# A list scheduler that knows a shared port, and gains moved from weights to activations

## The chip, the cores and the metric

The kernel runs on one core of one Trainium2 chip. Its engines work side by side, each with its own list of instructions in a fixed order: TensorE (PE) multiplies matrices, VectorE (DVE) and ScalarE (ACT) work on whole tiles, GpSimd (POOL) does the same more slowly, and SyncE (SP) issues the transfers. Instructions of different engines wait for each other by semaphores. The metric is the device time of one execution in microseconds (us). Lower is better.

## The reference

Two layers of a hybrid decoder over 1024 tokens of width 1024. Each layer normalises `x`, projects it once for four groups of heads, mixes, normalises each group, projects back, and then runs a gated feed-forward part of inner width 2816:

```python
def rmsnorm(x, gain):
    y = xf * lax.rsqrt(jnp.mean(xf * xf, axis=-1, keepdims=True) + NORM_EPS)
    return (y * gain.astype(jnp.float32)).astype(x.dtype)
...
for l in range(DEPTH):
    h = rmsnorm(x, norm_mix[l])
    (a_x, a_gate, b_q, b_kv, b_gate, c_q, c_k, c_v, c_glr, c_og,
     d_cq, d_ckv, d_kr) = jnp.split(h @ w_in[l], offsets, axis=-1)
    y_a = rglru_mixer(...); y_b = nsa_mixer(...)
    y_c = gla_mixer(...);   y_d = mla_mixer(...)
    y = jnp.stack([y_a, y_b, y_c, y_d], axis=2)
    y = rmsnorm(y, group_norm[l].reshape(N_GROUPS, GROUP_WIDTH)).reshape(B, S, MIX_WIDTH)
    x = x + y @ w_out[l]
    h = rmsnorm(x, norm_ffn[l])
    gate, up = jnp.split(h @ w_gate_up[l], 2, axis=-1)
    x = x + (jax.nn.silu(gate) * up) @ w_down[l]
return rmsnorm(x, final_norm)
```

`rglru` is a gated linear recurrence, `nsa` an attention over compressed, selected and recent keys, `gla` linear attention with a decay for each channel, `mla` attention with low-rank queries and keys.

## The kernel before

Everything is kept in tiles of 128 partitions; the 1024 tokens are eight tiles `t`. Matrix products in full precision are made of three passes: each operand is split in a rounded part and the rest (two instructions, a cast on ScalarE and a subtraction on VectorE, which writes `T`, `w`, `wu` or `h`), and three of the four products are summed in PSUM.

**Stages of a layer.** Start: `norm_stream` computes `hn` (the normalised tile, without the gain) on VectorE, TensorE transposes it (L464), and the first columns of `w_in` are applied (L607). Linear attention: `gla_levels` multiplies, for each tile and each of four levels, a decayed query `dq` with a mask of the heads into `Qz`, and for a fifth level into `Qb`; TensorE then forms the scores (L938, L935). Beside that other columns of `w_in` fill TensorE (L607). Then the stage of the sparse attention's keys: `blk` are the blocks of keys with a position vector added, for the compression (L1164), `ckvn` the normalised low-rank key, `kd` a rotated key that TensorE transposes (L1061, L1089). Then both attentions, the output projection (L1787) with the residual additions `x_res`, and the feed-forward part. That one saves products by forming sums and differences of blocks of weights and activations first (`utmp`, `qtmp`, `hn`, `h1`, `h6`, `h7`, on GpSimd and VectorE): its entry transposes the normalised `hn` (L1934), its long products are L2158, and the down projection is L2299 with the last piece in L2324.

**Gains.** A group of weights (`Weights`) may carry a gain; `refine` then multiplies the loaded tile `stg` by it on GpSimd, `stg<-stg,gn`, before it is split (for the group that is needed first, inside the split on ScalarE and VectorE). This holds the gain of the first norm for `w_in` and that of the group norms for `w_out`. The feed-forward norm applies its gain in the norm itself: `hn<-x_res,rstd,ps`, with the gain's row broadcast in a PSUM tile. The power -1/2 of each norm is a GpSimd instruction, `rstd<-ms,negh`.

**What sets the order.** The program runs through `Flow`, a list scheduler at build time. Streams (generators) yield the time from which they can go on; each instruction has a cost by hand for its engine: `D_` for VectorE, `P_` for GpSimd, `A_` for ScalarE, `f.pe` for TensorE. `run` takes whatever can start first on its clock and writes it out, so the engines' orders follow from these costs. `when` adds a fixed delay between two engines. Nothing in this clock ties VectorE to GpSimd. Nearly all instructions are recorded at one line, L254.

```python
    def run(self, until):
        while not until():
...
            for eng, q in self.ops.items():
                c = self.clk.get(eng, 0.0)
                for o in q:
                    r = when(o[3], eng)
...
                    key = (max(c, r + load), o[0], r, o[1])
...
                start = max(self.clk.get(eng, 0.0), key[2])
...
                self.clk[eng] = o[7].t = start + o[2]
```

## Time and profile before

| | us |
|---|---|
| three runs, median | 2597.49 |
| lowest, highest | 2597.26, 2599.34 |
| the profiled execution | 2599.47 |
| its span | 2597.7 |

| engine | busy us | share of the span |
|---|---|---|
| TensorE, matmul | 2515.2 | 97% |
| TensorE, weight load (overlaps) | 2129.9 | 82% |
| VectorE | 1925.3 | 74% |
| ScalarE | 1248.9 | 48% |
| GpSimd | 870.9 | 34% |

The mean granted clock of TensorE is 0.991. A high share of one engine says what bounds the kernel on average; where that engine stands idle is read from the stretches and from the timeline. A number in square brackets behind an instruction in the timeline is the idle time of its engine just before it, with what ended that. An instruction that is marked x2 or x3 is a row of that many.

### The profile page before, as it was taken

The numbers are of one execution on the slowest core, as the hardware profiler recorded it, in microseconds if no ns is written. First come the engines' busy times: TensorE is split into PE (matmuls) and PEld (weight loads), VectorE is DVE, ScalarE is ACT, GpSimd is POOL, SyncE is SP. The second block draws the span as 40 slices with busy tenths as digits, with TensorE's granted clock in tenths as the row PEclk, the third lists the DMA queues.
The fourth block names the chain that finished last, engine by engine and source line by source line (L and its number), as shares of the span: only waits on it lengthen the run. The fifth ranks groups of instructions, "written<-read, shape, count | busy, mean of one in ns | idle before, by whom it ended". The sixth has DMA issues, their size and how long they took to land. (4 is left out here: it accounts for less than half of the span.)

```text
span 2597.7 us, 37861 instructions
## 1 busy us (share of the span) xinstructions
PE 2515.2 (97%) x13502; PEld 2129.9 (82%) x13502; DVE 1925.3 (74%) x3668; ACT 1248.9 (48%) x2791; POOL 870.9 (34%) x820
## 2 busy tenths in 40 slices
PE   9999999998999999999999999999989999999998
PEld 8788978887888888778888888888878888887786
DVE  7976987787665665798769678867875665667976
ACT  5444577774333333444343455877653333334443
POOL 4530122233333333543225211222243333336522
PEclk9999999999999999999999999999999999999999
DMA  3011102212223323543310111031302323335522
GB/s 132 27 37 58 42 17 80 60 61 71 86 91 108 106 99 100 213 156 98 114 60 17 53 47 36 25 90 46 107 28 94 106 99 101 105 104 204 162 90 89
DMA packets 136556, 222.12 MB, mean 86 GB/s; under 512 B 13456, under 2 KB 83504, under 8 KB 133808
## 3 DMA queue, kind: packets, MB, share of 16 engines
q1 hardware_dynamic: 136368, 219.70, 25.7%
q8 instruction: 107, 1.75, 0.3%
q14 instruction: 81, 0.66, 0.1%
HBM read 161.99 MB, written 49.28 MB: 81 GB/s over the span
## 5 line engine op out<-in xcount | busy, mean ns | idle before, releaser
L2158 PE MATMUL ps<-T,wu 128*128 128x512 f32 (+1 forms) x2160 | 498.8, 386 | 1.0 <-DVE qtmp L254 0.9
L2158 PEld LDWEIGHTS ps<-T,wu 128*128 128x128 f32 x2160 | 400.7, 189 | 85.4 <-issue 1.3
L2158 PE MATMUL ps<-h,wu 128*128 128x512 f32 (+1 forms) x1656 | 386.4, 386 | 1.1 <-ACT ps L254 0.6
L2158 PEld LDWEIGHTS ps<-h,wu 128*128 128x128 f32 x1656 | 302.2, 188 | 70.0 <-ACT ps L254 0.8
L607 PE MATMUL ps<-w,T 128*128 128x256 f32 x2304 | 314.8, 291 | 8.2 <-DVE ckvn L254 5.7
L607 PEld LDWEIGHTS ps<-w,T 128*128 128x128 f32 x2304 | 290.2, 192 | 17.0 <-issue 9.7
L2299 PE MATMUL ps<-T 128*128 128x512 f32 x1176 | 275.6, 390 | 3.8 <-DVE x_res L254 3.8
L254 POOL TENSOR_TENSOR rstd<-ms,negh 128x1 f32<-128x1 f32 (+1 forms) x152 | 98.8, 651 | 510.7 <-DVE ms L254 495.8
L2299 PEld LDWEIGHTS ps<-T 128*128 128x128 f32 x1176 | 220.8, 188 | 52.4 <-DVE x_res L254 4.3
L254 POOL TENSOR_TENSOR utmp<-stg,stg 128x512 f32<-128x512 f32 x84 | 113.9, 1356 | 340.5 <-DVE wu L254 134.5
L254 ACT CAST wu<-stg 128x512 fp32r<-128x512 f32 x220 | 136.2, 619 | 190.1 <-PE ps L2158 80.2
L254 DVE TENSOR_TENSOR wu<-utmp,wu 128x512 fp32r<-128x512 f32 x134 | 109.9, 820 | 110.9 <-ACT wu L254 104.4
L1787 PE MATMUL ps<-w,T 128*128 128x512 f32 x768 | 190.9, 396 | 0.0
L254 DVE TENSOR_TENSOR wu<-stg,wu 128x512 fp32r<-128x512 f32 x214 | 178.7, 836 | 14.8 <-ACT wu L254 14.8
L254 DVE TENSOR_TENSOR x_res<-x_res,ps 128x512 f32<-128x512 f32 x224 | 143.4, 680 | 31.5 <-PE ps L2299 16.3
L1787 PEld LDWEIGHTS ps<-w,T 128*128 128x128 f32 x768 | 140.3, 188 | 26.8
L254 DVE TENSOR_TENSOR pts<-ps,pts 128x512 fp32r<-128x512 f32 x212 | 139.4, 685 | 21.2 <-ACT pts L254 20.6
L254 ACT CAST wu<-utmp 128x512 fp32r<-128x512 f32 x134 | 83.2, 621 | 115.6 <-POOL utmp L254 115.4
L254 POOL TENSOR_TENSOR stg<-stg,gn 128x1024 f32<-128x1024 f32 x48 | 94.6, 1978 | 130.4 <-DMA stg<-in_w_out_dram 59.8
L254 POOL TENSOR_TENSOR stg<-stg 128x512 f32<-128x512 f32 x88 | 130.0, 1497 | 3.5
L254 ACT CAST pts<-ps 128x512 fp32r<-128x512 f32 x212 | 117.4, 586 | 21.7 <-PE ps L1711 17.1
L254 POOL TENSOR_TENSOR utmp<-stg 128x512 f32<-128x512 f32 x48 | 67.6, 1409 | 175.2 <-DMA stg<-in_w_gate_up_dram 79.5
(380 smaller groups left out, 4927.4 us busy)
## 6 DMA issues: line engine op xcount, KB each, us to landing
stg<-in_w_gate_up_dram SPq DMA_DIRECT2D x88, 512.0 KB, 3.8
stg<-af SPq DMA_DIRECT2D x70, 512.0 KB, 3.6
af<-so SPq DMA_DIRECT2D x20, 1024.0 KB, 6.1
stg<-in_w_in_dram SPq DMA_DIRECT2D x36, 512.0 KB, 3.7
br<-in_w_down_dram SPq DMA_DIRECT2D x24, 512.0 KB, 6.2
af<-sg SPq DMA_DIRECT2D x20, 512.0 KB, 2.7
stg<-in_cmp_w_dram SPq DMA_DIRECT2D x16, 512.0 KB, 3.9
stg<-in_w_out_dram SPq DMA_DIRECT2D x16, 512.0 KB, 3.7
```

The lines of the kernel that those rows point to most:

```text
L254: o[4](*o[5], **o[6])
L607: PE.matmul(o[:, :256], lhsT=T[:, a, k, t * P:(t + 1) * P], rhs=g.of(k)[:, b, :], start=(k == 0 and i == 0), stop=(k == NK - 1 and i == 2))
L1787: PE.matmul(o, lhsT=T[:, a, 2 * u + k, t * P:(t + 1) * P], rhs=w.w[:, b_, k * 512:k * 512 + 512], start=(n == 0), stop=(n == 6 * len(us) - 1))
L2158: PE.matmul(bk[b, i][:, cs], lhsT=u[:, x, k * P:(k + 1) * P], rhs=H[n][:, y, k, cs], skip_group_check=True, start=(start and k == 0 and s ...
L2299: PE.matmul(o, lhsT=a[:, x, t * P:(t + 1) * P], rhs=b[:, y], skip_group_check=True, start=(new and s == 0), stop=(k == k0 + nk - 1 and s = ...
```

## The change

It has three parts. First, the scheduler's clock. Delays between engines follow the engine that finishes (`LAG`) and the one that waits (`MORE`); matmuls cost `mm(n)` or, in fp32, `mm4(n)`, in the place of constants by hand; a scan costs twice as much as before; and instructions of VectorE and GpSimd that use the port between them (`two` in `D_`, every `tensor_tensor` in `P_`) start on the clock only when the other engine's last such instruction is over. Second, the products `Qz` and `Qb` in `heads` go from GpSimd to VectorE. Third, the gains leave the weights: `refine` multiplies nothing, and the norm applies the gain in one `scalar_tensor_tensor` with a gain row that is loaded broadcast over the partitions (`gain_rows`; `gm` for the first norm, `grow` for the group norms). For this SP issues a load of 512 KB behind the first tile of `x`, and others later; the host stores `group_norm` in another order.

```diff
+LAG = {"DVE": 0.12, "ACT": 0.14, "POOL": 0.08, "PE": 0.19}
+MORE = {"PE": 0.03, "POOL": 0.06}
-        return x.t + (0.12 if x.eng == eng else 0.26 if eng == "PE" else 0.19)
+        return x.t + LAG.get(x.eng, 0.19) + MORE.get(eng, 0.0)
+def mm(n):
+    return (n + 32) / 2400
+def mm4(n):
+    return max(n / 1200 + 0.003, 0.112)
...
                     r = when(o[3], eng)
+                    if o[10]:
+                        r = max(r, self.port["POOL" if eng == "DVE" else "DVE"])
...
                 self.clk[eng] = o[7].t = start + o[2]
+                if o[10]:
+                    self.port[eng] = start + o[2]
...
     def D_(n, deps, func, *a, **k):
-        return f.do("DVE", 0.07 + n / 960, deps, func, a, k)
+        name = getattr(func, "__name__", "")
+        two = (name in ("tensor_tensor", "tensor_tensor_scan") and sbuf(a[1]) and sbuf(a[2])
+               or name == "scalar_tensor_tensor" and sbuf(a[1]) and sbuf(a[3])
+               or name in ("tensor_scalar", "tensor_copy") and sbuf(a[0]) and sbuf(a[1]) and n >= 64)
+        return f.do("DVE", 0.07 + n / 960, deps, func, a, k, None, two)
...
-                e = P_(n, [e, par["ev"]], G.tensor_tensor, sv, sv, g.unsqueeze(2).to_broadcast([P, k, n // k]),
-                       ALU.mult)
...
-        return r, P_(172, e, G.tensor_tensor, r[:, :n], ms[:, :n], negh[:, :n], ALU.pow)
+        return r, P_(172 if n == 1 else 400, e, G.tensor_tensor, r[:, :n], ms[:, :n], negh[:, :n], ALU.pow)
+    def gain_rows(g, src):
+        nc.sync.dma_start(g, src.partition_broadcast(P))
+        return g, f.dma(P * DM * 2)
...
-            tn = D_(600, e, V.tensor_scalar, hn, src, r[:, 0:1], None, ALU.mult)
+            tn = D_(1024, [e, gain[1]], V.scalar_tensor_tensor, hn, src, r[:, 0:1], gain[0], ALU.mult, ALU.mult)
...
-            te = f.pe(6 * 0.216)
+            te = f.pe(6 * mm(512))
...
             if t == 0:
+                gmix.extend(gain_rows(gp.tile([P, DM], F32, name="gm"), I["norm_mix"][0]))
                 f.add(params(0, par), 0, "par")
...
         def heads(Q, src, n, deps):
-            return P_(4 * n, deps, G.tensor_tensor, Q, src.unsqueeze(1).to_broadcast([P, 4, n]),
+            return D_(4 * n, deps, V.tensor_tensor, Q, src.unsqueeze(1).to_broadcast([P, 4, n]),
                       bdmask.unsqueeze(2).to_broadcast([P, 4, n]), ALU.mult)
...
-            e = D_(160, e, V.tensor_scalar, yn, y, r[:, 0:1], None, ALU.mult)
+            e = D_(256, [e, A["ggrp"][1]], V.scalar_tensor_tensor, yn, y, r[:, 0:1], A["ggrp"][0][:, grp // 2],
+                   ALU.mult, ALU.mult)
```

TensorE keeps its 1975 rows of the program; GpSimd goes from 615 to 487, VectorE from 3277 to 3304. Three places show what moves.

GpSimd in linear attention of layer 0, before (`Qz`, `Qb` are the products with the heads' mask, `stg` a weight tile) and then of the change (`ms`, `rstd` are the norms' mean squares and powers):

```order
L254 TENSOR_TENSOR Qz0_921<-dq_1083,bdmask_105 128x256
L254 TENSOR_TENSOR Qb_924<-d_1099,bdmask_105 128x512
L254 TENSOR_TENSOR stg_1112<-stg_1112,gn_128 128x1024
L254 TENSOR_TENSOR Qz1_922<-dq_1156,bdmask_105 128x256
L254 TENSOR_TENSOR Qz2_923<-dq_1173,bdmask_105 128x256
L254 TENSOR_TENSOR stg_1131<-stg_1131,gn_128 128x1024
L254 TENSOR_TENSOR Qz0_921<-dq_1210,bdmask_105 128x256
L254 TENSOR_TENSOR Qz1_922<-dq_1216,bdmask_105 128x256
L254 TENSOR_TENSOR Qz2_923<-dq_1265,bdmask_105 128x256
L254 TENSOR_TENSOR Qb_924<-d_1259,bdmask_105 128x512
```

```order
L275 MEMSET wbd_894 128x512
L275 TENSOR_TENSOR rstd_1380<-ms_1379,negh_94 128x4
L275 TENSOR_TENSOR rstd_1383<-ms_1382,negh_94 128x1
L275 TENSOR_TENSOR rstd_1532<-ms_1531,negh_94 128x4
L275 TENSOR_TENSOR rstd_1535<-ms_1534,negh_94 128x1
L275 TENSOR_TENSOR rstd_1707<-ms_1706,negh_94 128x4
L275 TENSOR_TENSOR rstd_1710<-ms_1709,negh_94 128x1
L275 TENSOR_TENSOR rstd_1885<-ms_1884,negh_94 128x4
L275 TENSOR_TENSOR rstd_1888<-ms_1887,negh_94 128x1
```

The products and the gain multiplications are gone from GpSimd's row, and the small powers stand one behind the other.

VectorE at the entry of the feed-forward part of layer 0, before and then of the change, from the last subtraction of the tile before to the norm of the last tile that TensorE transposes:

```order
L254 TENSOR_TENSOR stg3_7670<-ps_8018,hn_7732 128x512
L254 TENSOR_TENSOR h6_7680<-hn_7732,h6_7680 128x4x128
L254 TENSOR_TENSOR T_108<-stg3_7670,T_108 128x4x128 x2
L254 TENSOR_TENSOR h1_7684<-hn_7732,h1_7684 128x4x128
L254 TENSOR_TENSOR x_res_7532<-x_res_7532,ps_7976 128x512
L254 TENSOR_TENSOR h7_7676<-hn_7732,h7_7676 128x4x128
L254 TENSOR_TENSOR wu_8062<-stg_7749,wu_8062 128x512
L254 TENSOR_TENSOR wu_8074<-stg_7690,wu_8074 128x512
L254 TENSOR_TENSOR x_res_7532<-x_res_7532,ps_8040 128x512
L254 TENSOR_SCALAR ms_8083<-ss_8082 128x1
L254 TENSOR_TENSOR wu_8062<-utmp_7675,wu_8062 128x512
L254 SCALAR_TENSOR_TENSOR hn_7732<-x_res_7532,rstd_8084,ps_7726 128x1024
```

```order
L275 TENSOR_TENSOR stg3_7566<-ps_7937,hn_7651 128x512
L275 TENSOR_TENSOR x_res_7468<-x_res_7468,ps_7899 128x512
L275 TENSOR_TENSOR T_108<-stg3_7566,T_108 128x4x128 x2
L275 TENSOR_TENSOR h1_7580<-hn_7651,h1_7580 128x4x128
L275 TENSOR_SCALAR ms_7985<-ss_7984 128x1
L275 TENSOR_TENSOR x_res_7468<-x_res_7468,ps_7965 128x512
L275 TENSOR_TENSOR h7_7572<-hn_7651,h7_7572 128x4x128
L275 TENSOR_TENSOR wu_7989<-stg_7630,wu_7989 128x512
L275 SCALAR_TENSOR_TENSOR hn_7651<-x_res_7468,rstd_7986,ps_7615 128x1024
```

The first `x_res` has moved ahead of two `T` and `h1`, and of the `wu` additions one is left ahead of `hn` instead of three.

VectorE at the entry of the down projection of layer 0, before and then of the change, from the `x_res` additions (four of one group, of which the second piece shows the last two) to the `wu<-utmp` that TensorE's first product with that tile waits for:

```order
L254 TENSOR_TENSOR x_res_7532<-x_res_7532,ps_10995 128x512
L254 TENSOR_TENSOR x_res_7532<-x_res_7532,ps_11001 128x512
L254 TENSOR_TENSOR T_108<-utmp_7675,T_108 128x512
L254 TENSOR_TENSOR x_res_7532<-x_res_7532,ps_11008 128x512
L254 TENSOR_TENSOR x_res_7532<-x_res_7532,ps_11014 128x512
L254 TENSOR_TENSOR wu_8062<-stg_11019,wu_8062 128x512
L254 TENSOR_TENSOR T_108<-qtmp_7674,T_108 128x512
L254 TENSOR_TENSOR T_108<-stg3_7670,T_108 128x512 x2
L254 TENSOR_TENSOR T_108<-stg_11041,T_108 128x512
L254 TENSOR_TENSOR wu_8074<-utmp_7675,wu_8074 128x512
```

```order
L275 TENSOR_TENSOR x_res_7468<-x_res_7468,ps_10930 128x512
L275 TENSOR_TENSOR x_res_7468<-x_res_7468,ps_10936 128x512
L275 TENSOR_TENSOR T_108<-utmp_7571,T_108 128x512
L275 TENSOR_TENSOR wu_7989<-stg_10926,wu_7989 128x512
L275 TENSOR_TENSOR T_108<-stg3_7566,T_108 128x512
L275 TENSOR_TENSOR T_108<-qtmp_7570,T_108 128x512
L275 TENSOR_TENSOR T_108<-stg3_7566,T_108 128x512
L275 TENSOR_TENSOR T_108<-stg_10972,T_108 128x512
L275 TENSOR_TENSOR T_108<-utmp_7571,T_108 128x512
L275 TENSOR_TENSOR wu_7993<-stg_11019,wu_7993 128x512
L275 TENSOR_TENSOR T_108<-qtmp_7570,T_108 128x512
L275 TENSOR_TENSOR wu_7993<-utmp_7571,wu_7993 128x512
```

The four `x_res` now stand together, and behind them come one `T<-utmp`, one `wu<-stg` and one `T<-qtmp` more than before, all ahead of this `wu<-utmp` (the other `T<-utmp` stood among the `x_res` before).

## Rows read from the trace of the kernel before

**Rows 1.** The page, part 1: busy us (share of the span) xinstructions, by engine.

```profile
PE 2515.2 (97%) x13502; PEld 2129.9 (82%) x13502; DVE 1925.3 (74%) x3668; ACT 1248.9 (48%) x2791; POOL 870.9 (34%) x820
```

**Rows 2.** Waits of PE: line, releaser: us in total, times, longest us.

```profile
PE ps L2299 <- DVE wu L254: 7.9, 2, 4.0
...
PE ps L938 <- POOL Qz L254: 4.7, 8, 1.2
```

**Rows 3.** Stretches of 40 us: sum, busy per engine (xcount), PEclk, DMA share, GB/s.

```profile
40.00:80.00 40.00, 38.75 (x221) 31.68 (x221) 31.54 (x97) 18.51 (x45) 12.96 (x13) 1.00 0.20 60
80.00:120.00 40.00, 37.46 (x233) 30.92 (x232) 37.42 (x111) 14.48 (x64) 22.66 (x27) 1.00 0.03 10
680.00:720.00 40.00, 40.00 (x175) 32.63 (x174) 24.65 (x32) 12.77 (x22) 14.00 (x10) 1.00 0.30 99
1440.00:1480.00 40.00, 39.15 (x221) 32.34 (x220) 32.23 (x66) 19.74 (x42) 12.65 (x13) 1.00 0.10 34
```

**Rows 4.** Lines by form, GpSimd: shapes xcount | busy us, mean ns | idle before.

```profile
L254 POOL TENSOR_TENSOR stg<-stg,gn 128x1024 f32<-128x1024 f32 x48 | 94.6, 1978 | 130.4 <-DMA stg<-in_w_out_dram 59.8 <-DMA stg<-in_w_in_dram 48.1 <-DVE x_res L254 21.4
...
L254 POOL TENSOR_TENSOR Qz<-dq,bdmask 128x256 f32<-128x256 f32 x64 | 43.6, 685 | 72.5 <-DVE dq L254 48.4 <-PE ps L814 18.3 <-PE ps L607 3.2
```

**Rows 5.** Lines by form, VectorE, same columns.

```profile
L254 DVE SCALAR_TENSOR_TENSOR hn<-x_res,rstd,ps 128x1024 f32<-128x1024 f32 x16 | 20.4, 1278 | 5.1 <-POOL rstd L254 4.9
...
L254 DVE TENSOR_TENSOR kd<-k,kt 128x256 f32<-128x256 f32 x16 | 6.7, 417 | 0.0
...
L254 DVE TENSOR_SCALAR hn<-x_res,rstd 128x1024 f32<-128x1024 f32 x8 | 6.0, 748 | 0.1
```

**Rows 6.** Timeline in linear attention: start us, us, instruction.

```profile
81.01 2.04 POOL L254 TENSOR_TENSOR stg<-stg,gn 128x1024 f32<-128x1024 f32 x1 [1.02 <-ACT d L254]
...
81.22 1.99 DVE L254 TENSOR_TENSOR d<-b 128x128 f32<-128x128 f32 x1
```

**Rows 7.** Timeline of the start stage.

```profile
22.57 2.38 DVE L254 TENSOR_SCALAR hn<-xt,rstd 128x1024 f32<-128x1024 f32 x1
...
25.09 1.06 PE L464 MATMUL ps<-ident,hn 128*128 128x128 f32 x8 [2.20 <-DVE hn L254]
```

**Rows 8.** Timeline of the stage behind linear attention.

```profile
247.15 2.02 DVE L254 TENSOR_TENSOR blk<-X,par 128x504 f32<-128x504 f32 x2
...
249.70 1.62 PE L607 MATMUL ps<-w,T 128*128 128x256 f32 x6 [2.85 <-DVE ckvn L254]
...
259.26 4.52 POOL L254 TENSOR_TENSOR stg<-stg,gn 128x1024 f32<-128x1024 f32 x2
...
259.60 5.08 DVE L254 TENSOR_TENSOR blk<-X,par 128x504 f32<-128x504 f32 x2
...
267.25 0.30 PE L1089 MATMUL ps<-ident,kd 128*128 128x128 f32 x1 [1.75 <-DVE kd L254]
```

**Rows 9.** Timeline at the entry of the feed-forward part.

```profile
636.38 3.49 DVE L254 TENSOR_TENSOR T<-stg,T 128x512 fp32r<-128x512 f32 x2
...
640.39 0.68 DVE L254 TENSOR_TENSOR x_res<-x_res,ps 128x512 f32<-128x512 f32 x1
...
644.58 1.28 DVE L254 SCALAR_TENSOR_TENSOR hn<-x_res,rstd,ps 128x1024 f32<-128x1024 f32 x1 [0.44 <-POOL rstd L254]
...
646.00 1.94 PE L1934 MATMUL ps<-ident,hn 128*128 128x128 f32 x8 [5.82 <-DVE lamw L254]
```

**Rows 10.** The stretch of 40 us there, columns as in Rows 3.

```profile
640.00:680.00 40.00, 32.07 (x191) 28.36 (x191) 31.38 (x69) 19.19 (x37) 17.26 (x13) 0.91 0.13 40
```

**Rows 11.** Timeline at the entry of the down projection.

```profile
1096.94 4.02 DVE L254 TENSOR_TENSOR T<-stg,T 128x512 fp32r<-128x512 f32 x3
1097.09 1.64 POOL L254 TENSOR_TENSOR qtmp<-br 128x512 f32<-128x512 f32 x1 [0.63 <-DVE T L254]
...
1100.88 0.68 DVE L254 TENSOR_TENSOR wu<-utmp,wu 128x512 fp32r<-128x512 f32 x1
...
1101.61 4.71 PE L2299 MATMUL ps<-wu,T 128*128 128x512 f32 x11 [3.94 <-DVE wu L254]
```

More of the change, by code (lines that the diff above doesn't have):

```diff
@@ L535, in params, with norm_stream @@
                    cpos=pr[:, 21:53].rearrange("p (j lp) -> p j lp", j=2), s4n=s4n, s2p=s2p,
-                   halfb=halfb, wg2=wg2, glan=glan, done=e)
-    def norm_stream(ready, load, hp, bufs, done, ahead=NT):
+                   halfb=halfb, glan=glan, done=e)
+    def norm_stream(ready, load, gain, hp, bufs, done, ahead=NT):
         hs = Slots(bufs)
@@ L620, in start_stage @@
         evs = []
-        f.add(norm_stream(ready, load, hp, bufs, done, 1), 4, "start")
+        f.add(norm_stream(ready, load, gain, hp, bufs, done, 1), 4, "start")
         def evac(t, o, te):
```

147 lines of the change are left out of this document (76 added, 71 removed).

## The prediction

> **What bounds the kernel now.** I read the page's first part, then TensorE's busy share by stretches of 40 us, then TensorE's waits, and then the timeline at each place where it stood idle. TensorE is busy 2515.2 us of a span of 2597.7 [rows 1], so all its idle time together is 2597.7 - 2515.2 = 82.5 us. The change gives TensorE the same 1975 rows of work in another order, so everything to be won or lost lies in those 82.5 us and in the clock. In the long matrix products of the feed-forward part a stretch of 40 us holds 40.00 us of matmul [rows 3]: nothing can be won there, whatever VectorE and GpSimd do. The idle time lies at the joints: the start, linear attention, the stage behind it, the entry of the feed-forward part, the entry of the down projection, and the tail. At most of them the releaser is VectorE, and beside the late VectorE instruction stands a GpSimd instruction.
>
> That is the second thing to see. A VectorE subtraction of 128x128 took 1.99 us while GpSimd multiplied a 128x1024 weight tile by its gain for 2.04 us [rows 6], though a product of twice that size on VectorE takes 0.417 us [rows 5]. Behind linear attention two additions `blk` took 2.02 us by themselves and 5.08 us beside two gain multiplications of 4.52 us [rows 8]. The two engines do not overlap there; one stands behind the other. The Trainium skill says so too: SBUF — State Buffer, section "Who interferes with whom", has a VectorE instruction with two SBUF inputs and a GpSimd instruction that reads SBUF exclude each other for the whole instruction. The trace agrees with the times just given. The rule also speaks against one part of the change: a product moved to VectorE still has two SBUF inputs, and by the rule alone it would go on standing behind GpSimd; the sum would then hold +7 instead of -7 for linear attention, and be +3.5. The order of the change shows only small powers left on GpSimd there, so I keep this as a rival.
>
> **Gains leave the weights.** 48 multiplications on GpSimd go, 94.6 us of its time [rows 4]. GpSimd is busy only 34% [rows 1], so its own time is worth nothing; what counts is which VectorE instruction stood behind one of them where TensorE waited. I take the places one by one.
>
> Start: the norm of a tile took 2.38 us where an undisturbed one of the same form takes 0.748 [rows 5, 7], and TensorE then stood idle 2.20 us [rows 7]. Up to 2.38 - 0.75 = 1.6 us goes. Against it, the fused norm (with the gain in the same instruction) is dearer: the nearest row is the fused form of the feed-forward norm, 1.278 us against 0.748 [rows 5], so 0.53 us on the first tile's chain, and the load of the broadcast gain is queued on SP ahead of the first weights. I take -1 us, between -2 and +2. The other fifteen fused norms add 15 x 0.53 = 8 us to VectorE, beside matmuls that run without a gap; I cost these at nothing, and if that cover is gone they are in the upper end of the range.
>
> Behind linear attention: the second stall of each layer (1.75 us at 267 us, [rows 8]) follows the 5.08 us of `blk`; without the multiplications `blk` is 3.06 us shorter, more than the stall. The stall stands once in each layer, 3.5 us, with shorter ones behind it; I take -4, between -5 and 0. The stall before it, 2.85 us at 249.70 [rows 8], stays: there `blk` stands ahead of `ckvn` on VectorE with GpSimd idle, and the new order has the same two `blk` ahead of `ckvn`.
>
> **No GpSimd products in linear attention.** 64 products `Qz` of 0.685 us go from GpSimd [rows 4] to VectorE, with 16 `Qb` of twice the width. On VectorE the nearest row is a product of the same size, 0.417 us [rows 5], so 64 x 0.417 + 16 x 0.83 = 40 us, 20 us a layer. GpSimd keeps only the small powers there, as the order of the change shows. Linear attention covers eight stretches of 40 us, four a layer (the first, the fullest and the last of them stand in [rows 3]); TensorE's idle time in the eight is 12.5 us. Of it 4.7 us are eight waits for `Qz` itself [rows 2]; made directly behind `dq` on the same engine, `Qz` comes sooner by a hand-over and by 0.27 us. Of the other 7.8 us part follows VectorE instructions that stood behind GpSimd; I take 2.3. Together -7. The ends: all 12.5 us goes, or VectorE becomes the bound. In the fullest stretch VectorE is busy 37.42 of 40 us [rows 3]. GpSimd is busy 22.66 us in it [rows 3]; less two gain multiplications of 1.98 us that is 18.7 us, nearly all `Qz` and `Qb`, which at 0.417 for 0.685 come to 11.4 us on VectorE. Against that stands what VectorE lost behind the two gain multiplications, up to 2 x 1.98 = 4.0 us, and behind the products on GpSimd, which no row prices. With none of the latter given back VectorE needs 37.4 + 11.4 - 4.0 = 44.8 us for 40; with a third of the 11.4 given back, 41. I take +3.5 us a layer, +7, as the upper end.
>
> **The scheduler's clock.** This moves instructions everywhere, and two places matter.
>
> Entry of the feed-forward part: TensorE waits 5.82 us at 646.00 [rows 9], and as long in layer 1. It waits for the norm `hn`, at 644.58 [rows 9], which needs the residual addition `x_res`, which starts at 640.39 because two slowed additions of 3.49 us stood ahead of it [rows 9]. In the new order `x_res` stands ahead of those two, and only one `wu` addition is left ahead of `hn` instead of three. So the norm comes sooner by two `wu` of 0.68 us (undisturbed, [rows 11]) and by the 0.44 us that it waited for the power [rows 9]: 1.8 us a layer, -3.5 together, between -6 and 0.
>
> Entry of the down projection: TensorE waits 3.94 us at 1101.61 for one `wu` addition [rows 11], and 7.9 us in the two layers [rows 2]. In the new order three more VectorE instructions with both inputs in SBUF stand ahead of this `wu`, from the first `x_res` of the group on. One costs between 0.68 us alone and 4.02 / 3 = 1.34 us beside GpSimd [rows 11], so 2.0 to 4.0 us a layer; I take 2.5, +5 together. The ends are -2 (they run in time that VectorE idled before) and +8.
>
> The rest of the order I cost at nothing, because TensorE has no gap for it to fill.
>
> **The sum.** -1 - 4 - 7 - 3.5 + 5 = -10.5 us. The profiled execution took 2599.47 us, so it would be 2589.0 there; that execution lies 2.0 us above the median of 2597.49, so the forecast against the median is 2587.0.
>
> **The rivals.** First, the clock. The stretch of 40 us that holds the wait of 5.82 us has a mean granted clock of 0.91 [rows 10]. The two levels are 1.2 and 2.4 GHz, so 0.09 x 40 x 2 = 7.2 us of it went at the lower one, and 3.6 us were lost. Six such stretches stand in the trace, one a layer behind linear attention, at the feed-forward entry and at the down projection's entry. If shorter waits keep the clock up at four of them, 14 us go beside my 10.5, and the time is about 2573. For it: the stretch from 80 to 120 us holds 40.00 - 37.46 = 2.54 us of waits at a clock of 1.00 [rows 3], so short waits do not bring it down. Against it: by my own steps waits of 2.85, 4.1 and over 5 us stay, one in each of the six.
>
> Second, slower: VectorE becomes the bound of linear attention. It decides from the point where `Qz` and `Qb` cost more than the blocked time that they replace. Then +7 there; the down projection's entry at its upper end +8, as VectorE is the late engine there too; against -4 behind linear attention and -1 at the start. That is +10, 2607. For it: VectorE at 37.42 of 40 us [rows 3], and a product with both inputs in SBUF can still stand behind a power on GpSimd, as `blk` stood behind the gain multiplications [rows 8]. Against it: only one stretch a layer is that full. The Trainium skill's rule above (SBUF — State Buffer, "Who interferes with whom") stands behind this rival, not behind its price.
>
> Third, the change does not do what it says: a truer clock reorders engines that were off the critical path, TensorE's gaps only move, and the gain in linear attention is spent at the next joint. Then between -4 and +4, about 2597.
>
> **How the numbers follow.** Forecast 0.47, centred on 2587 (2578 to 2592); clock rival 0.14; nothing moves 0.18; slower 0.21. A measurement of this kernel can tell about 0.2%, 5.2 us, from no change, so faster means below 2592.3: 0.47 and 0.14, and a little of the third, 0.62. Same 0.17. Slower, above 2602.7, 0.21. The range reaches from the clock rival nearly to that of the slower one: 2570 to 2605.
>
> **What would show it.** `Qz` waits gone from TensorE's list and linear attention's stretches nearer 40.00: the largest term. `blk` at 2 us in both places: the second. The wait at the feed-forward entry near 4.1 us, that at the down projection's entry near 6.4. VectorE busy over 39 of 40 us in linear attention with TensorE waiting for `Qz` on VectorE would show the slower rival; slices at full clock behind the joints, the clock rival. A fault in the forecast would most likely be at the down projection's entry, where I read only the order and no time.

## The result

The changed kernel takes 2611.93 us (median of four runs, 2607.83 to 2615.82), the one before 2597.38. The ratio is 1.0054, with an interval of 1.0037 to 1.0072: it is slower, where I had forecast 2587.0. Its profiled execution is the lowest of the four, 2607.83 us, with a span of 2606.1 and a mean granted clock of 0.993; the other three lie at 0.988 to 0.991. So the two traces show 2606.1 - 2597.7 = 8.4 us of the difference. The other 6 us are that this execution lies 4.1 us below the median of its kernel, at the highest clock of the four, and the one before 2.1 us above its own.

The page's first part, by engine as in [rows 1]:

```profile
PE 2519.3 (97%) x13489; PEld 2123.4 (81%) x13489; DVE 1873.2 (72%) x3748; ACT 1249.0 (48%) x2791; POOL 734.4 (28%) x692
```

TensorE is idle 86.8 us, 4.3 more than before, and busy 4.1 us more. GpSimd lost 136 us of work, and VectorE 52 us, though it took over 37 us of products. The engines that were to be relieved are relieved, and the kernel is slower.

To find the place I cut both traces at the same instructions: the first transposed probabilities of the latent attention (L1504 before), the first transposes of the feed-forward entry (L1934), the first product of the down projection (L2299) and of its last piece (L2324). Times between these rows in the two timelines, in us:

| stretch | before | after | difference |
|---|---|---|---|
| layer 0, start to the latent attention | 333.9 | 328.9 | -5.0 |
| layer 0, both attentions and output projection | 267.3 | 278.2 | +10.9 |
| layer 0, feed-forward entry and products | 478.7 | 478.8 | +0.1 |
| layer 0, down projection | 200.4 | 199.7 | -0.7 |
| last piece and layer 1 to the latent attention | 339.7 | 333.1 | -6.6 |
| layer 1, both attentions and output projection | 268.1 | 279.0 | +10.9 |
| layer 1, feed-forward entry and products | 476.9 | 477.1 | +0.2 |
| layer 1, down projection to the end | 232.6 | 231.2 | -1.4 |

What I had worked out came in the sum: the two stretches with the start, linear attention and the stage behind it are 11.6 us shorter, for -12. What I had not worked out at all, the attentions, cost 22 us.

### The places of the prediction

Lines by form of VectorE in the changed kernel (shapes xcount, busy us, mean ns, idle before):

```profile
L275 DVE TENSOR_TENSOR Qz<-dq,bdmask 128x256 f32<-128x256 f32 x64 | 26.0, 419 | 0.0
...
L275 DVE TENSOR_TENSOR Qb<-d,bdmask 128x512 f32<-128x512 f32 x16 | 11.0, 686 | 0.0
```

`Qz` takes 0.419 us on VectorE, where I took 0.417 from [rows 5]; `Qb` 0.686 where I took 0.83. TensorE's list of waits holds no `Qz` any more (4.7 us in [rows 2]), though one wait of 2.3 us for `Qb` on VectorE is new. From the first product with `Qz` to the last output, linear attention takes 109.2 us in layer 0 and 114.3 in layer 1, for 115.2 and 115.6 before: 7.3 us less, for -7. The stretch of linear attention that was the fullest, columns as in [rows 3]:

```profile
80.00:120.00 40.00, 40.00 (x286) 36.82 (x285) 33.75 (x123) 13.35 (x56) 2.54 (x3) 1.00 0.08 26
440.00:480.00 40.00, 40.00 (x239) 34.08 (x238) 25.99 (x84) 28.55 (x78) 9.84 (x12) 0.96 0.36 109
```

VectorE went from 37.42 to 33.75 us in it, though the products were added. Over the whole of linear attention in both layers it is busy 188.5 us for 188.7: what it had lost behind GpSimd was about as much as the 37 us that it took over. The stretch from 440 us shows a mean clock of 0.96 inside the sparse attention; before, the clock came down at the joints and in the tail alone.

The stage behind linear attention, and the entry of the feed-forward part, from the timeline:

```profile
244.31 2.02 DVE L275 TENSOR_TENSOR blk<-X,par 128x504 f32<-128x504 f32 x2
...
246.87 0.95 PE L629 MATMUL ps<-w,T 128*128 128x256 f32 x6 [2.83 <-DVE ckvn L275]
...
254.85 2.19 DVE L275 TENSOR_TENSOR blk<-X,par 128x504 f32<-128x504 f32 x2
```

```profile
642.60 0.68 DVE L275 TENSOR_TENSOR x_res<-x_res,ps 128x512 f32<-128x512 f32 x1
...
643.20 3.10 DVE L275 TENSOR_TENSOR T<-stg,T 128x512 fp32r<-128x512 f32 x2
...
648.78 1.28 DVE L275 SCALAR_TENSOR_TENSOR hn<-x_res,rstd,ps 128x1024 f32<-128x1024 f32 x1
...
650.20 1.06 PE L1966 MATMUL ps<-ident,hn 128*128 128x128 f32 x8 [3.27 <-DVE ms L275]
```

The second pair of `blk` takes 2.19 us where 5.08 stood, the first stall of 2.83 us stays, and the second is gone, as forecast in both points [rows 8]. But three waits of some 0.8 us stand between 264 and 272 us, and from the end of linear attention to the latent attention layer 0 takes 2.2 us more than before and layer 1 5.0 less. At the feed-forward entry `x_res` stands ahead of the two `T`, and the first wait is 3.27 us where 5.82 stood [rows 9]. From the first transposes there to the first long product it is 47.15 us, where 48.83 stood: 1.7 us a layer for the 1.8 that I had worked out. The products behind it lose them again (431.7 us for 429.9, and 430.0 for 428.1), so the table shows +0.1 and +0.2 for the two together.

The entry of the down projection:

```profile
1104.48 0.62 ACT L275 CAST wu<-stg 128x512 fp32r<-128x512 f32 x1 [5.09 <-DMA stg<-af]
1105.00 0.61 ACT L275 CAST T<-utmp 128x512 fp32r<-128x512 f32 x1
...
1105.67 0.50 PE L2331 MATMUL ps<-T 128*128 128x512 f32 x1 [3.89 <-ACT T L275]
```

The wait is still 3.9 us (3.94 in [rows 11]), but another ends it: ScalarE's `T`, behind a `wu` cast that waited 5.09 us for a transfer. Of the nine VectorE instructions that now stand between the `x_res` and this `wu`, six run while ScalarE waits, and cost nothing; the other three run behind ScalarE's `T`.

### The place that I had not looked at

The latent attention, from its first transposed probabilities to its last product with the values, takes 88.3 us before and 96.0 after. First the stretch before and its largest waits among TensorE, ScalarE and VectorE (engine, line, releaser: us in total, times, longest), then the same of the changed kernel:

```profile
334.00:422.00 88.00, 84.82 (x596) 75.51 (x597) 76.81 (x192) 74.42 (x195) 20.53 (x40) 1.00 0.06 19
```

```profile
ACT Pm L254 <- DVE m L254: 2.8, 6, 1.0
...
DVE pts L254 <- ACT pts L254: 2.1, 7, 0.7
...
PE ps L1528 <- DVE pts L254: 0.9, 2, 0.5
```

```profile
329.00:424.00 95.00, 87.39 (x593) 75.67 (x593) 76.02 (x191) 73.16 (x194) 16.10 (x37) 1.00 0.05 18
```

```profile
ACT Pm L275 <- DVE m L275: 11.1, 11, 2.1
...
DVE pts L275 <- ACT pts L275: 8.0, 9, 1.4
...
PE ps L1559 <- DVE pts L275: 3.5, 5, 1.3
```

VectorE and ScalarE do the same work in both, some 76 and 74 us, and before the change each of the three engines is busy over 84% of the stretch. There is no free engine here: all three hand tiles to each other, and the order of each list decides who waits. ScalarE's wait for the row maximum `m` went from 2.8 to 11.1 us, VectorE's for the cast half of the probabilities from 2.1 to 8.0, TensorE's for the other half from 0.9 to 3.5. One such place:

```profile
385.39 1.05 ACT L275 CAST pts<-ps 128x512 fp32r<-128x512 f32 x2
...
386.30 1.21 DVE L275 CUSTOM_DVE_ANT_1 Pm<-ps,mask 128x1024 f32<-128x1024 f32 x1
...
387.44 0.86 DVE L275 TENSOR_TENSOR mq<-ps,mq 128x256 fp32r<-128x256 f32 x2
...
388.31 1.89 DVE L275 TENSOR_TENSOR pts<-ps,pts 128x512 fp32r<-128x512 f32 x3
...
389.06 1.22 PE L1559 MATMUL ps<-pts,VM 128*128 128x256 f32 x7 [1.32 <-DVE pts L275]
```

ScalarE has cast `pts` by 386.5 us, but on VectorE a row of scores with its maximum and two `mq` stand ahead of the subtraction, 386.30 to 388.31. TensorE waits 1.32 us. No instruction is slower here than elsewhere; the wait comes from the order of VectorE's list.

The sparse attention, from its first transposed probabilities to its last product, went from 145.0 to 150.1 us in layer 0 and from 144.8 to 150.9 in layer 1. There TensorE's idle time grew by 1.4 and 2.1 us only; its busy time, for the same products, went from 144.07 to 147.76 us in layer 0, part of it at the lower clock. I did not follow that to single waits.

### The profile page after: what moved, and what is told of

The parts are those of the page before. It is cut to its first block, busy times and chain, and to the rows that moved or that the text cites. A ratio compares the mean times of both kernels' runs of the same rounds, so it can differ in the third digit from the quotient of the medians.

```text
span 2606.1 us, 37563 instructions
## 1 busy us (share of the span) xinstructions
PE 2519.3 (97%) x13489; PEld 2123.4 (81%) x13489; DVE 1873.2 (72%) x3748; ACT 1249.0 (48%) x2791; POOL 734.4 (28%) x692
## 4 chain that ended last, share of the span: by engine, by line
PE 83%; DVE 8%; ACT 4%; issue 2%; DMA 1%; SPq 1%; POOL 1%; DVEq 0%; ACTq 0%; POOLq 0%
PE ps L2190 31%; PE ps L2331 14%; PE ps L629 7%; PE ps L1819 6%; PE ps L1368 3%; PE ps L614 3%; PE ps L1762 2%; PE ps L1743 2%; PE ps L686 2%; PE ps L2356 1%; PE ps L1559 1%; DVE T L275 1%; PE ps L968 1%; DVE w L275 1%; PE ps L1535 1%
## 5 line engine op out<-in xcount | busy, mean ns | idle before, releaser
L1819 PEld LDWEIGHTS ps<-w,T 128*128 128x128 f32 x768 | 140.1, 189 | 26.6
L275 DVE TENSOR_TENSOR wu<-utmp,wu 128x512 fp32r<-128x512 f32 x138 | 104.1, 754 | 78.8 <-ACT wu L275 77.7
L275 POOL TENSOR_TENSOR stg<-stg 128x512 f32<-128x512 f32 x88 | 138.3, 1590 | 3.4
L275 ACT CAST T<-stg 128x512 fp32r<-128x512 f32 x116 | 71.0, 621 | 102.5 <-PE ps L2331 88.2
L275 DVE TENSOR_TENSOR qtmp<-ps,qtmp 128x512 f32<-128x512 f32 (+1 forms) x92 | 61.2, 665 | 81.3 <-PE ps L2190 81.3
```

Source lines behind the costliest of these rows:

```text
L275: o[4](*o[5], **o[6])
L1819: PE.matmul(o, lhsT=T[:, a, 2 * u + k, t * P:(t + 1) * P], rhs=w.w[:, b_, k * 512:k * 512 + 512], start=(n == 0), stop=(n == 6 * len(us) - 1))
```

## The experiments

The change has three parts and the clock has three pieces (delays, port, costs of matmuls). Each was taken alone, then taken out, then put in alone. The stretches below are cut as above; "attentions" is the stretch with the output projection in layer 0 and 1, "products" the feed-forward entry and products.

| kernel | us | ratio to before, interval | attentions | products |
|---|---|---|---|---|
| before | 2597 to 2599 | | 267.3, 268.1 | 478.7, 476.9 |
| the changed kernel | 2611.93 | 1.0054 [1.0037, 1.0072] | 278.2, 279.0 | 478.8, 477.1 |
| clock_only | 2657.81 | 1.0223 [1.0206, 1.0241] | 276.9, 275.7 | 478.9, 477.7 |
| heads_only | 2601.56 | 1.0011 [1.0002, 1.0020] | 266.7, 267.1 | 478.7, 476.9 |
| gains_only | 2586.51 | 0.9952 [0.9937, 0.9966] | 268.7, 268.4 | 478.0, 476.2 |
| after_oldclock | 2578.71 | 0.9923 [0.9908, 0.9937] | 268.9, 268.7 | 478.0, 476.2 |
| after_oldlag | 2592.26 | 0.9976 [0.9966, 0.9985] | 273.9, 273.2 | 476.5, 477.8 |
| after_noport | 2670.78 | 1.0280 [1.0265, 1.0295] | 279.7, 282.3 | 504.1, 506.2 |
| after_oldmm | 2609.25 | 1.0045 [1.0030, 1.0060] | 271.2, 273.1 | 477.9, 477.3 |
| oldclock_lag | 2598.71 | 1.0003 [0.9993, 1.0012] | 271.1, 271.7 | 480.9, 477.1 |
| oldclock_port | 2598.30 | 1.0002 [0.9993, 1.0012] | 268.1, 268.9 | 478.6, 478.1 |
| oldclock_mm | 2668.19 | 1.0268 [1.0253, 1.0284] | 273.5, 276.0 | 516.9, 508.6 |
| after_slack | 2619.87 | 1.0083 [1.0068, 1.0098] | 272.9, 274.5 | 483.6, 482.2 |
| oldclock_jitter | 2577.18 | 0.9919 [0.9904, 0.9934] | 269.1, 268.3 | 478.0, 476.2 |
| oldclock_jitter2 | 2573.12 | 0.9906 [0.9889, 0.9922] | 267.7, 268.5 | 478.0, 476.2 |
| after_jitter | 2606.90 | 1.0032 [1.0018, 1.0045] | 279.5, 279.0 | 478.2, 477.1 |
| after_jitter2 | 2610.97 | 1.0044 [1.0029, 1.0059] | 279.5, 280.4 | 478.4, 477.0 |
| oldclock_ffcost | 2651.18 | 1.0188 [1.0158, 1.0217] | 269.0, 268.6 | 514.6, 509.7 |
| oldclock_attcost | 2598.42 | 0.9995 [0.9986, 1.0004] | 273.4, 276.3 | 480.5, 480.2 |
| after_oldlag_rest | 2604.32 | 1.0023 [1.0011, 1.0034] | 272.2, 273.4 | 477.6, 475.1 |

Two of them, after_oldmm and oldclock_port, write a wrong output. In these two alone GpSimd writes 22 of the sums for the down projection's weights into `qtmp` and 18 into `utmp`, where every other kernel has 20 and 20; which instruction then reads a wrong tile is not known. They run as many instructions as the others, so their times stand in the table, but neither could be used, and what rests on them is weaker for it.

### The three parts by themselves

The theories: A, the new clock writes a worse order for the attentions; B, the group norms with their gain row slow them; C, any new order moves them by chance.

clock_only is the kernel before with the hunks of `LAG`, `MORE`, `mm`, `mm4`, the port and the scan and power costs. 

> Only the scheduler's clock is changed: delays, matmul costs, scan and power costs, port. Gains stay in the weights and the products stay on GpSimd. Measured so far: from the first transposed probabilities of the latent attention to the entry of the feed-forward part the kernel before takes 267.3 us in layer 0 and 268.1 in layer 1, the changed one 278.2 and 279.0. Theory A (the new clock writes an order for both attentions that the chip runs worse): about 278 and 279 here too, and the whole 8 to 15 us slower than before, since the gains of the other two parts are missing. Theory B (the group norms' fused instruction with its gain row slows the attentions): 267 and 268, whole within 5 us of before. Theory C (any new order moves this stretch by chance): some other value, not within 3 us of either.

heads_only is the kernel before with one hunk:

```diff
-            return P_(4 * n, deps, G.tensor_tensor, Q, src.unsqueeze(1).to_broadcast([P, 4, n]),
+            return D_(4 * n, deps, V.tensor_tensor, Q, src.unsqueeze(1).to_broadcast([P, 4, n]),
```

> Only the products with the heads' mask go from GpSimd to VectorE; clock and gains as before. Theories A and B: the stretch of the attentions as before, 267 and 268 us; linear attention (first product with Qz to the last of its outputs, 115.2 and 115.6 us before, 109.2 and 114.3 in the changed kernel) shorter by 2 to 4 us; whole 4 to 8 us faster. Theory C: the stretch of the attentions moves by over 3 us in one layer at least, though nothing in it was changed.

gains_only has the third part alone: the changed kernel with the old clock and `heads` on GpSimd. 

> Only the gains move from the weights to the activations; clock and products as before. Theory A: attentions 267 and 268 us within 3, the stalls behind linear attention and in the start stage shorter, whole 4 to 10 us faster. Theory B: attentions 278 and 279, whole 5 to 12 us slower. Theory C: the attentions move by over 3 us to some other value.

after_oldclock is the changed kernel with the old clock; of its diff against the changed kernel the first hunks, the other costs likewise:

```diff
-        return x.t + LAG.get(x.eng, 0.19) + MORE.get(eng, 0.0)
+        return x.t + (0.12 if x.eng == eng else 0.26 if eng == "PE" else 0.19)
...
-                    if o[10]:
-                        r = max(r, self.port["POOL" if eng == "DVE" else "DVE"])
...
-                        te = f.pe(4 * mm(256))
+                        te = f.pe(0.44)
...
-                te[n, i] = f.pe(12 * mm(cs.stop - cs.start))
+                te[n, i] = f.pe(12 * 0.0025 + 12 * (cs.stop - cs.start) / 2400)
```

> The changed kernel with the old clock of the scheduler (delays, matmul, scan and power costs, no port): products on VectorE, gains in the norms. Theory A: attentions 267 and 268, linear attention and the start as in the changed kernel, whole 2580 to 2590. Theory B: attentions 278 and 279, whole 2600 to 2612. Theory C: the attentions at some other value, whole anywhere between.

Theory A holds for the attentions: 276.9 and 275.7 us with the clock alone, 268.7 and 268.4 with the gains alone, 268.9 and 268.7 with both other parts and the old clock. B is left with 1 to 2 us at most (latent attention 90.6 and 89.6 us in gains_only for 88.3 and 88.1). C does not show here: heads_only leaves the attentions within 1 us.

The sizes were off. The clock alone costs 59 us, not 8 to 15, and much of it in linear attention, which takes 132.5 and 140.1 us (from the first product with `Qz` to the last output) for 115.2 and 115.6: with products and gain multiplications still on GpSimd, TensorE waits for `Qz` on GpSimd and for what stands behind it on VectorE, and the clock falls with it, to a mean of 0.81 in the 40 us from 160 and 0.65 in those from 1480. heads_only won 2.5 us in linear attention of layer 0 and lost 6.8 in layer 1, where TensorE waits for `Qz` on VectorE:

```profile
1419.27 1.22 DVE L254 TENSOR_TENSOR w<-stg,w 128x1024 fp32r<-128x1024 f32 x1
...
1421.55 2.07 PE L938 MATMUL ps<-Qz,kt 128*128 128x256 f32 x4 [3.08 <-DVE Qz L254]
...
1421.94 1.89 POOL L254 TENSOR_TENSOR stg<-stg,gn 128x1024 f32<-128x1024 f32 x1 [8.70 <-DVE Qz L254]
1422.27 1.71 DVE L254 TENSOR_TENSOR d<-b 128x128 f32<-128x128 f32 x1
```

That is the rival "VectorE becomes the bound" in its direction. At this wait no gain multiplication runs yet; VectorE has worked without a gap since 1405 us, and two `w` of 1.2 us stand ahead of `Qz`. Right behind it the multiplications run, a `d` of 128x128 takes 1.71 us for 0.29, and TensorE waits 2.59 us more for `Qb`; the 40 us from 1400 stand at a mean clock of 0.83. Over linear attention VectorE is busy 202.0 us in heads_only, for 188.7 before and 188.2 with the gains gone as well (after_oldclock); there linear attention takes 105.6 and 108.8 us. So heads and gains belong together: gains alone win 12.3 us, heads alone lose 2.8, and both without the clock make the kernel 20.1 us faster than the before of the same runs (2598.78). That is the version to keep. The sign that I had named for this rival, VectorE over 39 of 40 us, does not stand in its linear attention: the fullest 40 us there have 37.38.

### The three pieces of the clock, taken out

Of the hunks shown for after_oldclock, after_oldlag takes the one with `LAG` and `MORE` out of the changed kernel, after_noport the one with `self.port`, and after_oldmm those with `mm` and the other costs of matmuls, scans and powers.

> The changed kernel with the old delays between engines alone (0.12, 0.19, 0.26 to TensorE); new matmul, scan and power costs and the port stay. With the whole old clock the kernel took 2578.7 us, with the whole new one 2611.9, so 33 us are to be divided. Theory D (the shorter delays, DVE or ACT to TensorE 0.15 to 0.17 where 0.26 stood, write consumers too close behind their producers): latent attention (first transposed probabilities to the last product with VM) back from 95.3 and 96.0 us to about 90, sparse attention (first transposed probabilities to the last product with VS) from 150 and 151 to about 145, whole 2580 to 2590. Theory E (port) and F (matmul costs): no change within 3 us in these stretches, whole 2605 to 2615.

> The changed kernel with the port taken out of the scheduler's clock alone; new delays and costs stay. Theory E (instructions that the port holds back on the clock lose their turn, and what comes in their place is late on the chip): latent attention back to about 90 us and sparse attention to about 145, whole 2580 to 2590. Theories D and F: no change within 3 us in these stretches, whole 2605 to 2615; linear attention, where GpSimd has almost nothing left, the same within 2 us under all three.

> The changed kernel with the old matmul, scan and power costs alone; new delays and the port stay. Theory F (the matmul costs set how far TensorE's list runs ahead of ScalarE and VectorE): latent attention back to about 90 us and sparse attention to about 145, whole 2580 to 2590. Theories D and E: no change within 3 us, whole 2605 to 2615. If each of the three gives back some 10 us, no single piece is the cause.

Theory D (delays) is the only one whose whole lies near what it expected, 2592.3 for 2580 to 2590, but the attentions come back by only 4.3 and 5.8 us of 11. The port was expected to do harm or nothing; without it the kernel is 59 us slower, and 54 us of that lie in the feed-forward products, which nobody had suspected. The old matmul costs give the attentions 7 and 6 us back and lose them again around linear attention and in the down projection (in a kernel with a wrong output). None of the theories covers this: the pieces work on each other.

### The three pieces, put in alone

Each is after_oldclock with one of the pieces above put back; after_slack is the changed kernel with

```diff
-MORE = {"PE": 0.03, "POOL": 0.06}
+MORE = {"PE": 0.12, "POOL": 0.06}
```

> Products on VectorE, gains in the norms, old matmul costs, no port; of the scheduler's clock only the delays are the new ones. Against the same kernel with the whole old clock, 2578.7 us, and the changed kernel, 2611.9. Theory D (the short delays are what costs time): latent attention 93 us, sparse attention 148, whole 2592 or more. Theory G (delays and matmul costs each do harm only where the port is missing, as the feed-forward products show, which took 457 and 459 us without it and 431 with it): feed-forward products about 457 here, whole 2630 or more.

> Products on VectorE, gains in the norms, old delays and matmul costs; of the scheduler's clock only the port is new. Theories D and G: the port does no harm by itself; attentions within 2 us of 90 and 145, whole 2574 to 2582, and perhaps the fastest of all. Theory E' (the port costs time in the attentions too): attentions 2 to 5 us longer, whole 2585 or more.

> Products on VectorE, gains in the norms, old delays, no port; of the scheduler's clock only the matmul, scan and power costs are new. Theory D: attentions within 2 us of 90 and 145, whole 2574 to 2584. Theory F (matmul costs alone): attentions at 93 and 148, whole 2590 or more. Theory G: feed-forward products some 457 us, whole 2630 or more.

> The changed kernel with one number: 0.12 instead of 0.03 is added to every delay to TensorE, which brings ScalarE and VectorE to TensorE back to 0.24 to 0.26; delays between the other engines stay short. Theory D1 (it is the slack ahead of TensorE, whose list runs in order, that was lost): at least half of the 20 us that the old delays gave back, whole 2602 or less. Theory D2 (it is the delays between ScalarE and VectorE): no gain, 2605 to 2615.

From 2578.7 the delays alone cost 20 us, the port alone 20, the matmul costs alone 89. The port loses them around linear attention (layer 0 326.6 us to the latent attention for 319.6; layer 1 337.5 for 331.7) and at the down projection (203.1 for 200.0, which the other kernel with a wrong output shows too, 202.7); it leaves the attentions alone. The matmul costs lose 39 and 32 us in the feed-forward products. With the port they lose nothing there (after_oldlag, which is oldclock_mm with the port, takes 476.5 and 477.8 us): the port repairs what the matmul costs break. Theory G held for the matmul costs and not for the delays, and its harmless port costs 20 us.

The changed kernel, after_oldclock and the six kernels with pieces taken out or put in are all eight combinations of the three pieces (two of them with the wrong output). With the port in, the new matmul costs change the time by -6.0 (old delays) and +2.7 us (new delays); without it by +89.5 and +72.1. The new delays cost 2.6 to 20.0 us in each of the four pairs.

More delay to TensorE alone does not help the whole (2619.9, above the range of either theory; D1 falls). But it gives the attentions back 5.3 and 4.5 us, about as much as the old delays, and loses more elsewhere: 11.2 us from the last piece to the latent attention of layer 1, 5 us in each layer's products.

### Is it the order's chance?

The old and the new clock, each with its delays moved by 1 or 2 ns, which is nothing on the chip but moves rows: 0.121, 0.259, 0.191 and 0.118, 0.262, 0.188 in the place of 0.12, 0.26, 0.19; `LAG` of 0.121, 0.139, 0.081, 0.191 and 0.118, 0.142, 0.078, 0.188 in the place of 0.12, 0.14, 0.08, 0.19.

> Products on VectorE, gains in the norms, the whole old clock, with its three delays moved by 1 ns (0.121, 0.259, 0.191). The order on TensorE changes in a few rows only. Theory K (the pieces of the new clock cost what they cost): 2575 to 2584. Theory H (chance of the order): a few rows change little either, so 2575 to 2590.

> As before, the three delays moved by 2 ns the other way (0.118, 0.262, 0.188), which moves many rows on TensorE and VectorE. Theory K: within 5 us of 2578.7. Theory H: 2588 to 2600, as far from 2578.7 as with the new delays or the port alone, in linear attention and the attentions above all.

> The changed kernel with its delays moved by 1 ns (0.121, 0.139, 0.081, 0.191). Theory K: within 5 us of 2611.9; latent attention 95 to 96 us, sparse attention 150 to 151. Theory H: anywhere from 2595 to 2630.

> The changed kernel with its delays moved by 2 ns (0.118, 0.142, 0.078, 0.188). Theory K: within 5 us of 2611.9. Theory H: anywhere from 2595 to 2630, and not where the 1 ns version lies.

The old clock gives 2578.7, 2577.2 and 2573.1, the new one 2611.9, 2606.9 and 2611.0: two groups, 28 us apart, each some 5 us wide. The attentions stay within 2 us of their own value in all six. For the two clocks Theory H falls. A single stretch moves more: the old clock takes 331.7, 328.3 and 324.8 us from the last piece to the latent attention of layer 1, and linear attention of layer 0 takes 109.2, 115.1 and 109.2 us with the new one. The pieces were each built once; their 20 to 89 us lie well outside the 5 us, but in which stretch the port loses its 20 is not clear of this scatter.

### Which costs, which delays

oldclock_ffcost is after_oldclock with the last hunk shown of its diff undone, oldclock_attcost with the costs of the attentions' matmuls undone, after_oldlag_rest the changed kernel with

```diff
-        return x.t + LAG.get(x.eng, 0.19) + MORE.get(eng, 0.0)
+        return x.t + (LAG.get(x.eng, 0.19) + MORE["PE"] if eng == "PE" else 0.12 if x.eng == eng else 0.19)
```

> Products on VectorE, gains in the norms, the old clock, with one cost changed: the twelve matmuls of a feed-forward unit at 12 x 544 / 2400 = 2.72 us in the place of 2.59. If this cost alone does it (the clock then lets VectorE's wu subtractions, which wait for ScalarE and GpSimd, stand ahead of the addition in PSUM that TensorE waits for): feed-forward products 457 to 470 us in both layers where 429 and 427 stood, attentions within 1 us of 90 and 145, whole 2640 or more. If it needs the other costs too: 430, whole within 6 us of 2578.7.

> Products on VectorE, gains in the norms, the old clock, with the new matmul costs in the two attentions alone. Theory F: latent attention 92 to 93 us in both layers where 90.7 and 89.5 stood, sparse attention 148 to 151 where 144.7 and 145.6 stood, feed-forward products as before, whole 2586 to 2595. If the attentions' loss comes from costs elsewhere: 90 and 145, whole within 6 us of 2578.7.

> The changed kernel with the old delays between all engines but TensorE (0.12 within an engine, 0.19 between); delays to TensorE stay at the new 0.11 to 0.17. All old delays gave back 20 us (2592.3), a longer delay to TensorE alone gave nothing (2619.9). Theory D2 (the delays among VectorE, ScalarE and GpSimd): 2590 to 2600. If it takes both kinds together: 2605 or more.

One number makes 72 of the 89 us. A unit of twelve matmuls at 2.72 us instead of 2.59 makes the feed-forward products 36.6 and 33.5 us longer and leaves nearly everything else as it was, as expected for the case that this cost alone does it. TensorE waits 20 times for one addition in PSUM, which it did not in after_oldclock, and in the stretches the clock falls (40 us of layer 0's products, first with the new cost, then with the old one):

```profile
PE ps L2188 <- DVE ps L273: 48.9, 20, 3.6
```

```profile
800.00:840.00 40.00, 37.78 (x159) 30.51 (x158) 22.66 (x30) 12.30 (x22) 14.17 (x10) 0.96 0.30 99
```

```profile
800.00:840.00 40.00, 40.00 (x175) 32.71 (x174) 25.71 (x32) 12.72 (x22) 14.88 (x11) 1.00 0.30 99
```

The waits are 48.9 of the 70 us. Another part is the clock: of the eight stretches from 680 to 1000 us seven stand at 0.96 to 0.99 with the new cost, where those of after_oldclock to 920 us all stand at 1.00. The four runs go the same way, 2636.0 us at a mean clock of 0.990 and 2649.8 to 2653.9 at 0.982 to 0.984.

One of the waits, and above it the engines that it hangs on:

```profile
695.04 0.69 DVE L273 TENSOR_TENSOR qtmp<-qtmp,ps 128x512 f32<-128x512 f32 x1 [0.77 <-ACT sg L273]
...
699.57 1.26 POOL L273 TENSOR_TENSOR utmp<-stg 128x512 f32<-128x512 f32 x1 [11.26 <-issue]
700.87 0.62 ACT L273 CAST wu<-utmp 128x512 fp32r<-128x512 f32 x1 [5.86 <-POOL utmp L273]
...
701.52 0.69 DVE L273 TENSOR_TENSOR wu<-utmp,wu 128x512 fp32r<-128x512 f32 x1 [5.79 <-ACT wu L273]
...
702.13 0.68 DVE L273 TENSOR_TENSOR wu<-stg,wu 128x512 fp32r<-128x512 f32 x1
...
702.73 0.69 DVE L273 TENSOR_TENSOR ps<-ps,qtmp 128x512 f32<-128x512 f32 x1
...
703.48 1.65 PE L2188 MATMUL ps<-h,wu 128*128 128x512 f32 x3 [3.58 <-DVE ps L273]
```

`ps<-ps,qtmp` on VectorE needs its `qtmp`, done at 695.7 us, and ScalarE's `sg` of the same bank, whose products TensorE ended at 697.1. Neither needs anything that is late. But the addition stands behind two `wu` on VectorE, the first of which waits 5.79 us for ScalarE; on ScalarE two `wu` stand ahead of that `sg` too (it starts at 701.91), and the first waits 5.86 us for GpSimd's `utmp`. That began 0.12 us after a transfer of weights landed, at 699.45 us, which SP had issued at 691.30. All four engines stand still for it. In layer 0's products GpSimd waits for such transfers 14 times:

```profile
POOL utmp L273 <- DMA stg<-in_w_gate_up_dram: 123.8, 14, 10.2
```

The two lists of VectorE differ in this, at one such place (+ is the new cost, - the old one):

```
+L273 TENSOR_TENSOR wu_8021<-utmp_7634,wu_8021 128x512
+L273 TENSOR_TENSOR ps_8595<-ps_8595,qtmp_7633 128x512
 L273 TENSOR_TENSOR wu_8021<-stg3_7629,wu_8021 128x512
-L273 TENSOR_TENSOR ps_8595<-ps_8595,qtmp_7633 128x512
-L273 TENSOR_TENSOR wu_8021<-utmp_7634,wu_8021 128x512
```

With the old cost the addition stands ahead of the subtraction that hangs on GpSimd, with the new one behind it. Then the addition waits for `sg` alone, as VectorE's waits with the old cost show; with the new cost this row is gone:

```profile
DVE ps L273 <- ACT sg L273: 19.9, 10, 2.0
```

VectorE's wait for ScalarE's `wu` in layer 0's products is 133.6 us in 73 places with the new cost and 48.3 in 21 with the old one.

The attentions' matmul costs alone make latent attention 92.8 us in both layers (90.7 and 89.5) and sparse attention, from its first transposed probabilities to its last product, 148.5 and 151.5 (144.7 and 145.6): Theory F, in both layers. The whole, 2598.4, lies above its range, since the feed-forward stretch is 2.5 and 4.0 us longer too. The delays between the engines other than TensorE give the attentions back 6 us a layer, but the whole comes only to 2604, between the two theories: 2592 takes both kinds of delay.

## Why the prediction was wrong

**The parts that I priced** came out in the sum. Start, linear attention and the stage behind it, -12 in the sum, are -11.6 in the changed kernel. Part of that is luck: a stretch there moves by up to 7 us with delays that differ by 1 or 2 ns, and the layers share the 11.6 otherwise than I had it. With the old clock they are -22 (319.6 us for 333.9, and 331.7 for 339.7): linear attention alone 9.6 and 6.8 us, where I took 3.5 a layer. What no row priced, VectorE's time behind the `Qz` on GpSimd, is the likely reason: VectorE took over 37 us of products and is busy no longer in linear attention than before. The first stall behind linear attention stayed, the second went and shorter ones came. The feed-forward entry gave 1.7 us a layer for 1.8, and the products behind it took them back.

**The down projection**, +5 in the sum, is -0.7 and -1.4: I counted instructions ahead of the late `wu` and did not ask whether VectorE or ScalarE is late there. In the new order ScalarE was, behind a transfer.

**The step that failed** is one sentence: "The rest of the order I cost at nothing, because TensorE has no gap for it to fill." That holds for gains. A stretch in which TensorE is hardly ever idle has nothing to win, but it can lose: 22 us in the attentions (TensorE was busy 84.82 of 88 us in the latent attention before), and in after_noport 54 us in the products, [rows 3]'s 40.00 of 40 us. So the sentence that everything to be won or lost lies in the 82.5 us of idle time was wrong for losses. It also took TensorE's busy time as fixed: the same 598 matmuls of the latent attention stand at 85.1 us of busy time before and 88.3 after. I bounded what the reordering could win and not what it could lose, and that term, put at nothing, measured +22 us, more than all the others together.

**The rivals.** "The change does not do what it says" was nearest, and its price of 4 us was far off. "VectorE becomes the bound" gave nearly the right time, 2607, by luck: something like it shows in heads_only, not in the changed kernel. The clock rival was half right. Of the six stretches at 0.91 two stand at 1.00 now (behind linear attention), two at 0.96 and two at 0.91 still, and three new ones stand at 0.96 (from 440, 1600 and 1720 us), two of them in the sparse attention. The runs of the changed kernel, 8 us apart, are the longer the lower their clock.

**The Trainium skill's rule** (SBUF — State Buffer, "Who interferes with whom") holds as far as the traces show it: `blk` 5.08 us beside GpSimd, 2.19 without. The warning that I drew from it, products that go on standing behind GpSimd, did not come true: none of the 64 `Qz` took longer than 0.434 us, with nearly nothing left on GpSimd there.

**What stays open.** The new numbers are the truer ones: 175 matmuls in 40.00 us of the products [rows 3] are 0.229 us each, for which the new clock has 544 / 2400 = 0.227 and the old one 0.216; and TensorE starts 0.14 us after `hn` at 645.86 us [rows 9], for which the new clock has 0.15 and the old one 0.26. Why truer numbers give worse lists is shown at one place only: with the longer unit the lists put what TensorE waits for behind a `wu` that the chip delivers late (a transfer, then a GpSimd instruction), and an engine that works its list in order stands still. The times on the scheduler's clock were not recorded, so that it believed this `wu` to be ready is argued. For the attentions the cause stays open. Longer delays to TensorE, longer delays among the others, all the old delays, and the old matmul costs each give back 4 to 7 of the 11 us a layer; that the old numbers act as slack there is argued, not shown.

## What to carry to other kernels

Where a planner sets the order, a change of its costs has to be priced in every stage, above all in those that run without a gap: they have little to win and much to lose. Test the planner's numbers apart from the code that they are changed with; here two good edits of 20 us were hidden under a third that cost 33. And look in each engine's list for what stands first and waits: one instruction behind a late one, with everything at hand, can stop four engines.

## What the runs showed of the hardware

On VectorE the 64 products of 128x256 took between 0.409 and 0.434 us each, and the 16 of 128x512 0.686 us in the mean. With the long GpSimd products gone, VectorE's whole busy time fell by 52 us while its list grew by 80 instructions. TensorE's granted clock also fell where no wait was long: from 440 us of the changed kernel it stands at 0.96, and no wait of the 40 us before was over 0.8 us. In the products of oldclock_ffcost it stands at 0.96 behind waits of up to 3.6 us. Over the whole kernel the short waits cost no more clock than the long ones had: the changed kernel's runs stand at 0.988 to 0.993, those of the one before at 0.989 to 0.993.
